# Tensor, vector and scalar engine of a streaming-encoder mixer: from program order to the scheduler's order

## Chip, cores, metric

The kernel runs on one core of a Trainium2 chip. The metric is the device time of one execution in microseconds (us); the time of a kernel is the median of several runs.

## What is computed

The reference is one hybrid encoder block on 1024 frames of width 1024 with 16 learned meta tokens in front, all in float32. A token mixer of eight heads (four mLSTM heads, four retention heads) is followed by a gated MLP with a causal convolution:

```
h = concat(meta, x)
u = rmsnorm(h) ; proj = u @ w_in          # q, k, v, output gate of 4 + 4 heads
q, k: convolution + silu (mLSTM)  or  rotary (retention)
per chunk of a head:  out = (q k^T * decay) v + q C ;  C = decay * C + k^T v
h = h + (gate * head_norm(out)) @ w_out
h = h + (silu(dwconv(rmsnorm(h) @ w_up)) * (rmsnorm(h) @ w_gate)) @ w_down
out = rmsnorm(h)[16:]
```

The state C makes the nine chunks of a head a serial chain; the heads are independent of one another.

## The kernel before, in words

**Stages.** The norm of the input, the projections of head 4's value and query and the sums of activation blocks come first. Then the mixer runs over the heads in the order 4, 0, 1, 2, 3, 5, 6, 7, three pairs after the first head (line 1521, `for p, (a, b) in enumerate(PAIRS)`). The output projection, the gated MLP and the final norm follow.

**The projections.** A projection of a head is a unit of seven block products (a Strassen-like scheme, `wino_fm` at L742 and `v_steps` at L788). Each product is split in chunks; one step is 12 matmuls of a group (L671 high weight times high input, L672, L673) into a PSUM bank of tag `pa` or `pb` (two banks each), and the bank is then copied out or added by `evac` (L734: ACT at L736 and L738, DVE at L740). A unit has 14 such evacuations. A float32 weight is used as a high and a low part: ACT casts the high part (L292), DVE subtracts for the low part (L295), after DVE has made sums of weight quarters (L368, L369, L372, L373).

**The scan.** For each chunk, `scan_a` (L1248) makes the scores on PE (L1255, L1260), then ACT scales the keys (L1271) and DVE the scores (L1274 to L1279). `scan_b` (L1282) makes state update and numerator on PE (L1302, L1304, L1306), then DVE updates the state (L1315), ACT copies the numerator out (L1317) and DVE takes its statistics (L1321). `post_steps` (L1325) normalises with a square root on ACT (L1340, L1342) and L1350, transposes on PE into the one bank `tr` (L1359), multiplies by norm weight and gate on DVE into one of three buffers `mx` (L1367) and stores that to DRAM (L1379, SP). The banks `sA`, `num`, `upd` and `tr` exist once each.

**Emission.** The order in which the program is written down is itself a plan. `slot` (L1417) emits one projection step and then up to two side tasks (scan pieces, convolutions, gates, table work), as long as estimated loads of DVE and ACT are not too far ahead of PE's; `tick` (L257) emits the evacuations of the step before and one piece of each pending weight split; `drain` (L1432) emits what is left of a head before its buffers are used again. `m_unit` (L396) folds two rows of the output weights and adds the result to DRAM (L420 on SP, L422 on POOL); its raw buffer is one of the four into which all later weights are loaded (L222, SP).

**Who orders the engines.** Line 2203 builds the program with `schedule_with_timeline_sim=True`: the framework's scheduler walks the emitted program over a modelled timeline, and an engine whose earliest instruction isn't ready there may take a later one that is. The resulting order is fixed at compile time; on the chip each engine follows it. A hook (L91 to L97) sees every instruction as it is emitted:

```
    def watch(ins):
        nm, kind = ins.engine.name, type(ins).__name__
        if nm not in RATE or not ins.outs or "DMA" in kind or "Tile" in kind:
            return
        if pinned[0] and nm in before:
            tc.add_manual_dep(ins, before[nm], mybir.DependencyInfo(mybir.DependencyClass.NoSync, mybir.DependencyReason.DATA), reason="order")
        before[nm] = ins.name
```

`RATE` names PE, DVE and ACT. While `pinned[0]` is true, each instruction of these engines depends, for its order alone and with no semaphore, on the one emitted before it on its engine: the engine keeps the order of emission. The rest of the hook keeps the load estimates and doesn't look at `pinned`. DMA issues on SP and POOL and the POOL memsets (L801) are never held.

`pinned[0]` is set true at L1520, after the seven products of head 4's output gate with head 4's first side tasks (`go(o_steps(4))`, L1519), and false at L1601, after the last scan of head 7 and the first six of the output projection's steps (`drain("end")`, L1599). All before L1520 and after L1601 goes by the scheduler's order.

Of the kernel before, what the change touches and what calls it, by code (L numbers as in the profile page):

```python
# [65 lines left out]
def body(ctx, tc, h_in, vecs, cst, mask_in, rot, w_v0, w_vp, w_g, w_out, w_up, w_gate, w_down, out):  # L66
# [19 lines left out]
    pinned = [False]  # L86
# [686 lines left out]
    def o_steps(h):  # L773
        return wino_fm("o", h, OC, fm_dst([sigt[:, 0], sigt[:, 1]], KEEP))
# [653 lines left out]
    def go(steps, pe=1):  # L1428
        for m in steps:
            slot(m, pe=pe)  # L1430
# [86 lines left out]
        return [(lambda: tables_load(h), 0, lambda: "gates" in done)]  # L1517
    reset()
    go(o_steps(4))  # L1519
    pinned[0] = True  # L1520
    for p, (a, b) in enumerate(PAIRS):
        side += sig_tasks(prev) if p else sig_tasks(4)
        side += rest[0] + loads_of(a)
# [684 lines left out]
```

## Time and profile before

| | |
|---|---|
| time, median of 3 runs | 1673.84 us (1672.29 to 1673.98) |
| the profiled execution's own time | 1665.56 us |
| its span, first to last instruction | 1663.6 us |
| PE busy | 1520.7 us, 91% |
| DVE busy | 1131.5 us, 68% |
| ACT busy | 761.0 us, 46% |
| mean granted TensorE clock | 0.961 |
| DMA moved | 232.16 MB, mean 140 GB/s |

The profile is of one execution. Busy time of an engine is the time in which it had an instruction; PE's own ends are modelled. The views used below are: busy time of each engine by stretches of the span; the sums of waits, where a row `PE tr L1359 <- DVE mx L1367: 23.7, 11, 6.3` says that PE's instruction of line 1359 writing `tr` stood idle until line 1367 on DVE had ended, 23.7 us in 11 cases, the longest 6.3; and the timeline, which gives start, duration, engine, line, operation, tiles (out<-in) and in square brackets the idle time before an instruction with its releaser. SPq is the queue of DMA issues on SP. The part of the span with held order lies between about 121 us (end of L1519's steps) and about 837 us.

### The profile page before, as it was taken

Reading aid. Unit: us, or ns where it says so; the run is one execution under the profiler, and the core shown is the slowest. Engines: PE = TensorE matmul, PEld = TensorE weight load, DVE = VectorE, ACT = ScalarE, POOL = GpSimd, SP = SyncE. Lnnn points to the kernel's source line nnn. Section 1 sums busy time; section 2 is a strip of 40 time slices with the busy share of each in tenths; the row PEclk is TensorE's granted clock in tenths of the full one; section 3 lists DMA queues with packets and bytes.
Section 4 is the critical chain, followed back from the end, with each engine's and each line's share of the span. In section 5 each row is a group of like instructions: output and inputs, shape, how many; then the busy total and the mean of one; then the engine's idle time right before and its main releaser. Section 6 shows DMA issues by size and latency. Waiting matters only on the chain.

```text
span 1663.6 us, 25278 instructions
## 1 busy us (share of the span) xinstructions
PE 1520.7 (91%) x9799; PEld 1375.4 (83%) x9799; DVE 1131.5 (68%) x2161; ACT 761.0 (46%) x1494; POOL 67.5 (4%) x104
## 2 busy tenths in 40 slices
PE   5988897798987999989779999999999999999998
PEld 4878786697986998888658899899999999888887
DVE  6685666566765776766377777877666666677757
ACT  5344543454563444454324545644444444444444
POOL 0000000000000000000000000022221000000000
PEclk9999998999998999999979999999999999999999
DMA  6013235442453425459644321788776222863312
GB/s 213 26 52 103 64 111 161 109 153 77 106 186 84 162 85 159 129 180 318 231 151 132 120 89 66 233 212 211 205 191 162 82 76 77 294 213 108 99 53 102
DMA packets 107175, 232.16 MB, mean 140 GB/s; under 512 B 10808, under 2 KB 34048, under 8 KB 106880
## 3 DMA queue, kind: packets, MB, share of 16 engines
q1 hardware_dynamic: 96736, 201.12, 36.6%
q0 software_dynamic: 10176, 29.37, 9.2%
q8 instruction: 76, 1.25, 0.3%
q14 instruction: 43, 0.35, 0.1%
q10 hardware_dynamic: 144, 0.07, 0.0%
HBM read 179.10 MB, written 74.49 MB: 152 GB/s over the span
## 4 chain that ended last, share of the span: by engine, by line
PE 69%; DVE 10%; DMA 8%; ACT 7%; issue 5%; SPq 0%; DVEq 0%; POOLq 0%; ACTq 0%
PE pdx L671 2%; PE pdx L672 2%; PE pdx L673 2%; PE pup_x L672 2%; PE pup_x L673 2%; PE pga_x L672 2%; PE pup_x L671 2%; PE pga_x L673 2%; PE pga_x L671 2%; PE pdy L672 2%; PE pdy L671 2%; PE pdy L673 2%; PE pwx L673 2%; PE pwx L671 2%; PE pwx L672 2%
## 5 line engine op out<-in xcount | busy, mean ns | idle before, releaser
L575 ACT CAST hi_up<-raw_up 128x512 fp32r<-128x512 f32 (+1 forms) x52 | 36.4, 719 | 106.0 <-PE pga_z L672 61.2
L671 PE MATMUL pup_x<-uh_g,hi_up 128*128 128x256 f32 (+1 forms) x240 | 67.1, 282 | 1.2 <-ACT uh_g L1612 1.2
L576 DVE TENSOR_TENSOR lo_ga<-fraw_ga,hi_ga 128x512 fp32r<-128x512 f32 (+1 forms) x52 | 41.9, 808 | 37.6 <-ACT hi_ga L575 37.4
L672 PE MATMUL pup_x<-ul_g,hi_up 128*128 128x256 f32 (+1 forms) x240 | 67.1, 281 | 0.1
L1321 DVE BATCH_NORM_STATS2 bn<-n 128x6 f32<-128x256 f32 (+1 forms) x72 | 30.8, 428 | 53.1 <-ACT den L1319 33.6
L673 PE MATMUL pup_x<-uh_g,lo_up 128*128 128x256 f32 (+1 forms) x240 | 66.4, 282 | 0.0
L576 DVE TENSOR_TENSOR lo_up<-raw_up,hi_up 128x512 fp32r<-128x512 f32 (+1 forms) x52 | 41.2, 808 | 35.7 <-ACT hi_up L575 34.9
L576 DVE TENSOR_TENSOR lo_d<-rd,hi_d 128x1024 fp32r<-128x1024 f32 (+1 forms) x34 | 37.7, 1112 | 32.9 <-ACT hi_d L575 32.8
L672 PE MATMUL pdx<-ul_d,hi_d 128*128 128x512 f32 (+1 forms) x156 | 58.1, 375 | 0.0
L673 PE MATMUL pdx<-uh_d,lo_d 128*128 128x512 f32 (+1 forms) x156 | 57.6, 373 | 0.0
L575 ACT CAST hi_ga<-fraw_ga 128x512 fp32r<-128x512 f32 (+1 forms) x52 | 36.4, 719 | 46.3 <-PE pup_z L672 24.0
L575 ACT CAST hi_d<-rd 128x1024 fp32r<-128x1024 f32 (+1 forms) x34 | 32.3, 960 | 49.0 <-PE pdy L672 32.6
L672 PE MATMUL pdy<-ul_d,hi_d 128*128 128x512 f32 x132 | 51.9, 393 | 0.0
L673 PE MATMUL pdy<-uh_d,lo_d 128*128 128x512 f32 x132 | 51.3, 389 | 0.0
L671 PE MATMUL pdx<-uh_d,hi_d 128*128 128x512 f32 (+1 forms) x156 | 48.8, 374 | 0.0
L671 PE MATMUL pdy<-uh_d,hi_d 128*128 128x512 f32 x132 | 48.3, 392 | 0.0
L672 PE MATMUL pga_x<-ul_g,hi_ga 128*128 128x512 f32 x120 | 47.6, 397 | 0.0
L673 PE MATMUL pga_x<-uh_g,lo_ga 128*128 128x512 f32 x120 | 47.3, 394 | 0.0
L671 PEld LDWEIGHTS pup_x<-uh_g,hi_up 128*128 128x128 f32 x240 | 45.3, 189 | 2.3 <-ACT uh_g L1612 1.4
L671 PE MATMUL pga_x<-uh_g,hi_ga 128*128 128x512 f32 x120 | 47.1, 393 | 0.0
L672 PEld LDWEIGHTS pup_x<-ul_g,hi_up 128*128 128x128 f32 x240 | 45.4, 189 | 1.1 <-DVE ul_g L1613 0.3
L673 PEld LDWEIGHTS pup_x<-uh_g,lo_up 128*128 128x128 f32 x240 | 44.6, 188 | 0.8
(1679 smaller groups left out, 5892.5 us busy)
## 6 DMA issues: line engine op xcount, KB each, us to landing
raw_up<-w_up_d SPq DMA_DIRECT2D x22, 512.0 KB, 4.4
fraw_ga<-w_gate_d SPq DMA_DIRECT2D x22, 512.0 KB, 4.2
acts<-cv SPq DMA_DIRECT2D x44, 256.0 KB, 4.1
wsd<-w_down_d POOLq DMA_DIRECT2D x44, 256.0 KB, 6.2
rd<-wsd SPq DMA_DIRECT2D x22, 512.0 KB, 3.6
raw_w<-w_out_d SPq DMA_DIRECT2D x20, 512.0 KB, 4.8
wsw<-raw_w SPq DMA_DIRECT2D x32, 256.0 KB, 3.9
raw_m<-w_out_d SPq DMA_DIRECT2D x14, 512.0 KB, 3.7
```

Source lines behind the costliest of these rows:

```text
L575: AC.copy(hi[:, o:o + n], x)
L576: V.tensor_tensor(lo[:, o:o + n], x, hi[:, o:o + n].bitcast(F32), ALU.subtract)
L671: m.append(PE.matmul(pt, ah, xh_, start=first and k == 0, stop=False, skip_group_check=True))
L672: PE.matmul(pt, ah, xl_, start=False, stop=False, skip_group_check=True)
L673: m.append(PE.matmul(pt, al, xh_, start=False, stop=last and k == n - 1, skip_group_check=True))
L1321: V.bn_stats(sb[:L], pn[:L, :DV])
```

## The change

One word. The order of emission, the load estimates that steer it, all operands, buffers and DMAs stay.

```
     go(o_steps(4))
-    pinned[0] = True
+    pinned[0] = False
     for p, (a, b) in enumerate(PAIRS):
```

With it the three engines get the scheduler's order in the whole program.

## Prediction

> **What bounds the kernel now.** I read the page first, then busy time by stretches, then what PE waited for inside the part whose order is held (121 to 837 us), and last the timeline around single stalls. The page:
>
> ```profile
> span 1663.6 us, 25278 instructions
> ...
> PE 1520.7 (91%) x9799; PEld 1375.4 (83%) x9799; DVE 1131.5 (68%) x2161; ACT 761.0 (46%) x1494; POOL 67.5 (4%) x104
> ```
>
> PE is the bound. Busy time by stretches (us of the stretch, then busy time of PE, weight loads, DVE, ACT, POOL, the granted clock, DMA):
>
> ```profile
> 121.00:837.00 716.00, 621.74 (x4456) 579.99 (x4455) 462.83 (x1030) 335.65 (x726) 11.62 (x20) 0.94 0.47 143
> ...
> 837.00:1663.00 826.00, 808.80 (x4685) 711.01 (x4685) 582.13 (x964) 371.81 (x679) 55.55 (x79) 0.99 0.48 143
> ```
>
> After the mixer PE is idle for 17.2 of 826 us, in the mixer for 716 - 621.74 = 94.3 of 716, or 13.2%, and its clock is 0.94 there against 0.99. Everything that the change can move lies in these 94.3 us and in what new idle time it makes: PE's work stays 621.74 us. What ended PE's waits there, in total, times, longest:
>
> ```profile
> PE tr L1359 <- DVE mx L1367: 23.7, 11, 6.3
> PE s L1255 <- ACT kT L911: 11.3, 4, 4.1
> PE n L1304 <- DVE bn L1321: 9.6, 6, 4.4
> PE pq5x L671 <- ACT hi_o L292: 9.3, 1, 9.3
> PE pq2x L671 <- ACT hi_o L292: 8.3, 1, 8.3
> PE v L842 <- ACT n L1263: 8.1, 1, 8.1
> ...
> PE po6y L671 <- DVE sig L740: 0.2, 1, 0.2
> ```
>
> The reader is to see two things. The waits are few and long, and they come from places where one head ends and the next begins. And the projections hardly wait for their banks to be emptied: po6y's 0.2 us is one of the two such rows, both 0.2. By the code the held part has 18 units with 14 evacuations each, 252 in all, so a handoff of a bank costs PE 0.4 / 252, nothing.
>
> **The change part by part.** It adds and removes no instruction, no DMA and no semaphore by itself; it lets PE, DVE and ACT take a later instruction where the scheduler's timeline finds the earlier one not ready. That has a good side and a bad side, and each is priced from a place of this trace.
>
> *What is given back.* An engine held to order stands still while later work is ready behind the waiting instruction. DVE near 373 us:
>
> ```profile
> 372.58 0.62 DVE L1367 SCALAR_TENSOR_TENSOR mx<-tr,vec,sig 128x384 f32<-128x384 f32 x1 [1.12 <-PE tr L1359]
> 378.90 0.62 DVE L1367 SCALAR_TENSOR_TENSOR mx<-tr,vec,sig 128x384 f32<-128x384 f32 x1 [5.70 <-DMA mxd<-mx]
> 379.43 1.22 DVE L368 TENSOR_TENSOR raw_vp<-raw_vp,raw_vp 128x1024 f32<-128x1024 f32 x1
> ```
>
> For 5.70 us DVE waits until a store has freed one of the three mx buffers, and only then makes the weight sum of L368 that stood behind. Set free, it would make the sum first, and PE would run projection steps while a transpose waits for the bank tr. I count the row tr <- mx, 23.7 us, as what can be filled, because projection matmuls with weights already split follow those transposes, and take three quarters of it: -18 us. The waits for kT, bn and n (11.3 + 9.6 + 8.1 us) are links of a serial chain with casts of the same moment behind them; pq5x and pq2x (9.3 + 8.3 us) wait for a weight that is still being loaded into a buffer which the accumulation into DRAM has to leave first:
>
> ```profile
> SPq L222 <- DMA accd<-raw_m: 106.6, 12, 23.0
> ```
>
> That is a matter of SP's and POOL's queues. Their order isn't held before either, but it comes from the same modelled timeline, so it moves with the engines: an accumulation that is ready earlier there goes out earlier, or a load is queued behind a store that is late. I bound this by these two waits on the one side (-17.6) and by one more wait as long as the longest of the row on the other (+23.0), and take 0, since both signs have the same ground. If all six rows quoted above went, it would be 70.3 us; with PE at the clock of the later stage the mixer would save another 621.74 x 0.05 = 31 us. That is the far end of the good side, -101; its near end is 0.
>
> *What it costs.* The trace holds a place where the same kind of work already runs in the scheduler's order: head 4's output gate, 75 to 121 us, with side tasks between its steps. PE's waits there:
>
> ```profile
> PE po4x L671 <- ACT sig L736: 3.7, 1, 3.7
> PE po4x L671 <- DVE sig L740: 3.1, 2, 2.2
> PE po4x L672 <- DVE uS2l L1494: 1.4, 1, 1.4
> ```
>
> The first two rows are the handoff of a bank, 6.8 us for the unit's 14 evacuations, 0.49 us each, against nothing in the held part. Why, is seen in the order. PE takes one matmul of the third product (uS2h) ahead of the second and the first product's other chunk:
>
> ```profile
> 88.73 0.28 PE L671 MATMUL po4x<-uS2h,hi_o 128*128 128x258 f32 x1
> 88.86 0.28 PE L671 MATMUL po4y<-u12h,hi_o 128*128 128x256 f32 x1
> ...
> 90.39 0.36 PE L671 MATMUL po4x<-u11h,hi_o 128*128 128x256 f32 x1
> ```
>
> and ACT fills its time with casts, one of them for the next head (raw_q0a), in front of the copy that empties PE's bank:
>
> ```profile
> 92.22 1.28 ACT L954 ACT_TABLE_LOAD   x1
> 93.52 0.36 ACT L954 ACTIVATE gates<-pg,gsm 36x128 f32<-36x128 f32 x1
> 93.78 0.60 ACT L292 CAST hi_o<-raw_o4a 128x512 fp32r<-128x512 f32 x1
> 94.29 0.62 ACT L292 CAST hi_o<-raw_q0a 128x512 fp32r<-128x512 f32 x1
> 94.81 0.61 ACT L292 CAST hi_o<-raw_o4a 128x512 fp32r<-128x512 f32 x1
> 95.33 0.36 ACT L736 COPY sig<-po4x 128x256 f32<-128x256 f32 x1
> ```
>
> ```profile
> 91.74 0.28 PE L673 MATMUL po4x<-u11h,lo_o 128*128 128x256 f32 x1
> 95.74 0.38 PE L671 MATMUL po4x<-uS2h,hi_o 128*128 128x256 f32 x1 [3.72 <-ACT sig L736]
> ```
>
> The bank was full at 92.0 and emptied at 95.7. Where the modelled timeline has the end of a matmul group later than the chip, or a cast earlier, an evacuation is put behind long foreign pieces (0.6 us a cast, 1.28 a table load), and in the fixed order it stays there. DVE was busy for 41.76 of the 46 us between 75 and 121, and that is what makes such a place dear: nine of the 48 stretches of 15 us between 120 and 840 have DVE busy 12 us or more; the first and the last of them:
>
> ```profile
> 210.00:225.00 15.00, 15.00 (x120) 14.68 (x119) 12.47 (x26) 6.89 (x17) 0.00 (x0) 1.00 0.12 36
> ...
> 750.00:765.00 15.00, 14.08 (x115) 13.66 (x115) 14.08 (x25) 5.49 (x12) 0.00 (x0) 1.00 0.75 268
> ```
>
> In them I price an evacuation as in the freed place: 252 x 9 / 48 = 47 of them by 0.49 us, +23 us. The other 205 lie between 0 (the held rows) and 0.49 us (the freed ones); I take a fifth, 0.1 us, nearer to the held rows, since DVE and ACT have spare time there: +20 us. Ends of the bad side: 0 and 252 x 0.49 = +123. The handoffs of the scan (two for each of 72 chunks) get no price of their own: their waits in the held part are in the rows above, and late copies of the numerator are the same mechanism.
>
> *Sum.* -18 + 0 + 23 + 20 = +25 us on the profiled execution's 1665.56 us, that is 1690.6. That execution lies 8.3 us under the median of the runs, 1673.84; the forecast is of a median, so **1673.8 + 25 = 1699 us**.
>
> [...]
>
> **The rivals.**
>
> *Faster: standing time is given back and little is lost.* For it speaks that every long wait above has ready work behind it, and that the stage after the mixer runs in the scheduler's order with PE idle for 2% only. Against it speak the rows of head 4's output gate, and that the later stage has no serial scan. It decides once less than 18 us are lost to late evacuations. With the first three rows and v given back by half (52.7 / 2 = 26), and nothing lost: 1673.8 - 26 = **1648 us**; with all six rows and the clock it could reach 1573, which I don't believe because of the serial chains.
>
> *No change: the order hardly differs.* If on the modelled timeline the held instructions are seldom late, the free choice picks the same ones. For it: the emission is already spaced by estimated loads. Against it: the order at 88.73 shows that the choice is used. **1674 us**.
>
> *Much slower: functions of ACT are mixed.* The square roots of the statistics come in 24 pieces (8 heads, 3 each) and now cost 11 loads:
>
> ```profile
> L1340 ACT ACT_TABLE_LOAD x6 | 7.7, 1283 | 0.1
> ...
> L1342 ACT ACT_TABLE_LOAD x5 | 6.4, 1283 | 0.1
> ```
>
> If free choice sets each between exponentials and silus, it takes a load for it and one back: 48 x 1.283 = 62 us on ACT, 48 more than now with 7 of the other loads counted in. ACT is busy 335.65 of 716 us, so half of it may be hidden: +24 beside the +25, and with evacuations at 0.2 us instead of 0.1 another +20: 1673.8 + 69 = **1743 us**. For it: ACT's order at 92.22, a load in front of the evacuation. Against it: the pieces of one function are emitted in one go.
>
> **How the numbers follow.** Forecast 0.52, much slower 0.20, faster 0.20, no change 0.08. The forecast's own spread is 1678 (5 us net) to 1730 (a third of the 123 more). The lower end of the range is 1652, which leaves out about half of the faster case, 0.11; the upper end 1765, half way between much slower and the +123 with the queues' +23 and half of the 62, leaves out about 0.08. A change of 0.2% (3.3 us) is about what a measurement of this kernel can tell from none. Faster by more than that 0.20, within it 0.08, slower 0.72.
>
> **What would show it.** Right: in the stretch of the mixer PE's idle time rises from 94 to about 119 us; the waits of PE for sig, raw, v (L736, L738, L740) rise from 0.4 to some 40 us; the row tr <- mx falls to about 6; table loads in the mixer stay near those now. Wrong: PE's waits for evacuations stay under 10 us (then the bad side was mis-sized), tr <- mx doesn't fall (then nothing was in hand behind it), or the idle time goes to weights that SP's queue brings late, which would make the queues' 0 the failed term. If the order on the engines turns out nearly that of before, the premise fails.

## The result

The changed kernel takes **1600.7 us** (median of 4 runs, 1598.8 to 1605.5) against 1673.1 us before: a ratio of 0.957, 95% interval 0.955 to 0.960. The forecast was 1699 us, slower, with a range of 1652 to 1765. The sign was wrong and the time lies outside the range.

### The profile after

The page of the changed kernel, the lines that answer to those shown of before:

```profile
span 1603.7 us, 25323 instructions
...
PE 1511.2 (94%) x9799; PEld 1368.9 (85%) x9799; DVE 1112.6 (69%) x2161; ACT 778.6 (49%) x1506; POOL 67.5 (4%) x104
```

The matmuls are the same 9799. ACT has 12 instructions more, all of them table loads. Busy time by stretches (stretch, PE, weight loads, DVE, ACT, POOL, granted clock, DMA):

```profile
121.00:777.00 656.00, 610.80 (x4461) 570.72 (x4460) 443.40 (x1030) 353.85 (x742) 11.53 (x20) 0.97 0.49 151
777.00:1603.00 826.00, 808.93 (x4706) 712.26 (x4704) 585.06 (x968) 372.60 (x679) 55.64 (x79) 0.99 0.49 144
```

The stage behind the mixer is as long as before, 826 us with 808.9 busy. The mixer took 716 us and takes 656: the whole difference of the two spans, 59.9 us, is there (777 us is set so that the rest is as long as before). PE's idle time in it fell from 94.3 to 45.2 us (49 us), and its busy time from 621.7 to 610.8 us (11 us) with the clock up from 0.94 to 0.97. (The medians are 72 us apart; the profiled execution of before lies 8 us under its median and that of after 5 us above.) What PE waits for now, us in total, times, longest:

```profile
PE n L1304 <- DVE bn L1321: 7.6, 5, 3.2
PE u L1302 <- DVE C L1315: 7.2, 2, 4.2
PE pwy L672 <- DVE rr L1030: 6.7, 1, 6.7
PE n L1304 <- DVE z L1336: 6.3, 3, 3.9
PE pq2x L671 <- ACT hi_o L292: 3.5, 1, 3.5
PE pq0x L671 <- ACT rawq L736: 3.5, 1, 3.5
...
PE pq5x L671 <- ACT hi_o L292: 0.8, 1, 0.8
...
PE tr L1359 <- DVE mx L1367: 0.5, 1, 0.5
```

The row that led before, tr <- mx with 23.7 us, is 0.5 us. The two waits for the weights of heads 5 and 2, 9.3 and 8.3 us, are 0.8 and 3.5. New is a row such as pq0x <- rawq, 3.5 us: a bank not yet emptied. All waits of PE from 121 us to the first MLP matmul (980 us before, 921 after), sorted by what PE was about to do (matmuls of a projection that waited for a weight part, or for a bank; transposes into tr; scan pieces; the output projection):

| PE waits, us | before | after |
|---|---|---|
| weights of the projections | 23.6 | 4.3 |
| banks of the projections | 0.4 | 9.5 |
| bank tr | 28.4 | 5.6 |
| scan pieces | 35.4 | 23.6 |
| output projection | 9.5 | 10.0 |
| other | 3.9 | 0 |
| sum | 101.2 | 52.9 |

How a weight came late is seen on ACT around head 2's first weight. Before, ACT's timeline:

```profile
322.40 0.37 ACT L736 COPY sig<-po1x 128x256 f32<-128x256 f32 x1 [1.08 <-PE po1x L673]
333.05 0.62 ACT L292 CAST hi_o<-raw_q2a 128x512 fp32r<-128x512 f32 x1 [10.27 <-DMA raw_q2a<-w_g_d]
```

For 10.27 us ACT stood at this cast; the scan's copies behind it stood too (the next numerator was complete at 323.7 us and was copied out at 334.09). After:

```profile
302.47 1.28 ACT L778 ACT_TABLE_LOAD   x1
303.77 1.06 ACT L778 ACTIVATE sig<-sig 128x1026 f32<-128x1026 f32 x1
304.73 0.35 ACT L736 COPY sig<-po1x 128x256 f32<-128x256 f32 x1
305.12 1.06 ACT L778 ACTIVATE sig<-sig 128x1026 f32<-128x1026 f32 x1
306.08 0.36 ACT L1317 COPY v<-n 128x256 f32<-128x256 f32 x1
...
310.44 0.20 ACT L1340 ACTIVATE z<-z 128x4 f32<-128x4 f32 x1
313.99 0.62 ACT L292 CAST hi_o<-raw_q2a 128x512 fp32r<-128x512 f32 x1 [3.34 <-DMA raw_q2a<-w_g_d]
```

ACT fills the time with two sigmoid passes, scan copies and a square root, and the cast comes when the weight is there. The load itself is issued 19.9 us sooner by the clock; SP's queue before, then after:

```profile
328.37 0.33 SPq L222 DMA_DIRECT2D raw_q2a<-w_g_d  x1
```

```profile
308.46 0.33 SPq L222 DMA_DIRECT2D raw_q2a<-w_g_d  x1
```

Seen from PE this weight comes no earlier, though: PE ends the unit before it, po1, 21.2 us sooner too (303.9 against 325.1), and starts pq2 10.8 us after that end, 8.6 before. PE's wait is shorter, 3.5 us against 8.3, because PE has scan matmuls in the first 7 us of the gap, while ACT copies the scan's numerators out. For head 5 the weight does come earlier: pq5 starts 2.2 us after po3's end, 10.6 before.

What the load waits for is the accumulation of the folded output weights into DRAM, whose buffer it takes (SP's queue stood for it 21.9 us before and 5.2 us after). The accumulation is issued on POOL, before and then after:

```profile
322.84 1.95 POOL L422 DMA_DIRECT2D accd<-raw_m  x2 [37.46 <-DVE raw_m L416]
```

```profile
303.19 0.87 POOL L422 DMA_DIRECT2D accd<-raw_m  x1 [0.85 <-DVE pt L1274]
```

The load follows it by 5.5 and 5.3 us, so the queues add the same in both kernels. Before, POOL stood until DVE's part of the fold (L416) was done.

### The profile page after: what moved, and what is told of

The parts are those of the page before. It is cut to its first block, busy times and chain, and to the rows that moved or that the text cites. A ratio compares the mean times of both kernels' runs of the same rounds, so it can differ in the third digit from the quotient of the medians.

```text
span 1603.7 us, 25323 instructions
## 1 busy us (share of the span) xinstructions
PE 1511.2 (94%) x9799; PEld 1368.9 (85%) x9799; DVE 1112.6 (69%) x2161; ACT 778.6 (49%) x1506; POOL 67.5 (4%) x104
## 4 chain that ended last, share of the span: by engine, by line
PE 71%; DMA 12%; DVE 9%; issue 4%; ACT 4%; SPq 0%; POOL 0%; DVEq 0%; POOLq 0%; ACTq 0%
DMA accd<-raw_m 3%; PE pdx L671 3%; PE pdx L672 3%; PE pdx L673 3%; PE pup_x L672 2%; PE pup_x L673 2%; PE pga_x L672 2%; PE pup_x L671 2%; PE pga_x L673 2%; PE pga_x L671 2%; PE pdy L672 2%; PE pdy L671 2%; PE pdy L673 2%; PE pwx L672 2%; PE pwx L671 2%
## 5 line engine op out<-in xcount | busy, mean ns | idle before, releaser
L575 ACT CAST hi_d<-rd 128x1024 fp32r<-128x1024 f32 (+1 forms) x34 | 32.3, 960 | 48.9 <-PE pdy L672 32.6
```

Of the source, the lines that this page charges most:

```text
L575: AC.copy(hi[:, o:o + n], x)
```

## The experiments

All ratios are to runs of the kernel before on the same chip; the medians come from several chips, so the ratios are what is compared. Theory A: the standing time sat on ACT and DVE. Theory B: PE's own freedom makes the gain. Theory C: all share it.

### One engine held, two free

The hook holds only the engines named:

```
-        if pinned[0] and nm in before:
+        if pinned[0] and nm in before and nm in ('PE',):
```

**PE held.** 

> PE alone is held to the order of emission in the mixer; DVE and ACT are free. Theory A (the standing time sits on ACT and DVE, whose waiting instruction keeps ready casts, sums and copies behind it; PE only suffers): most of the 72 us gain stays, 1610 to 1625 us. Theory B (PE's own freedom to run projection steps while a transpose or a scan piece is late makes the gain): most is lost, 1650 to 1670 us. Theory C (the engines share it, the gains do not add up): 1630 to 1645 us.

**DVE held.** 

> DVE alone is held. Theory A: DVE's waits for ACT and for the store buffers hold weight sums again, 1635 to 1660 us. Theory B: nearly as fast as with all free, 1600 to 1612 us. Theory C: 1625 to 1645 us.

**ACT held.** 

> ACT alone is held. Theory A: casts that wait for a load keep copies and evacuations behind them again, 1635 to 1660 us. Theory B: nearly as fast as with all free, 1600 to 1612 us. Theory C: 1625 to 1645 us.

### One engine free, two held

**PE free.** 

> PE alone is free in the mixer, DVE and ACT are held. Theory D (a weight goes from its load through ACT's cast and DVE's sums and back to the queue of loads, so ACT and DVE only help when both are free; PE alone can't shorten that chain): 1668 to 1685 us. Theory E (what a free PE takes early is evacuated late by engines that keep to the order of emission): slower than with one more engine free, 1690 to 1710 us. Theory B (PE's own freedom counts): 1640 to 1655 us.

**DVE free.** 

> DVE alone is free, PE and ACT are held. Theory D: little, 1665 to 1680 us. Theory E: the same, since PE keeps the order for which the other engines are placed. If each engine gave its own share (the 72 us in three parts): 1645 to 1655 us.

**ACT free.** 

> ACT alone is free, PE and DVE are held. Theory D: little, 1665 to 1680 us. Theory E: the same. If each engine gave its own share: 1645 to 1655 us.

Measured, all eight cases:

| free | median us | ratio, 95% interval |
|---|---|---|
| none (before) | 1673 | 1 |
| PE | 1714.4 | 1.025 (1.022 to 1.029) |
| DVE | 1681.2 | 1.006 (1.004 to 1.008) |
| ACT | 1662.1 | 0.994 (0.990 to 0.998) |
| PE, DVE | 1692.4 | 1.010 (1.007 to 1.013) |
| PE, ACT | 1689.4 | 1.007 (1.005 to 1.009) |
| DVE, ACT | 1640.1 | 0.978 (0.975 to 0.982) |
| all (after) | 1600.7 | 0.957 (0.955 to 0.960) |

No theory had this table. One free engine alone is worth little (ACT, 0.6%) or less than nothing. By the ratios ACT and DVE together bring 2.2%, and PE, which alone costs 2.5% and beside ACT 1.3%, brings another 2.1% once both are free. Theories A and B fall as written; C named the size with PE held (1630 to 1645) but not that holding DVE or ACT alone would end above the kernel before. D and E expected the same for DVE and ACT, little, and both times lie just outside their 1665 to 1680 us, so these two runs do not tell them apart. For PE, E's direction came out (its 1690 to 1710 was 4 us low), and its reason was tested next. With ACT held, PE's waits:

```profile
PE pwx L671 <- ACT hi_w L575: 12.7, 2, 12.3
PE pq5x L671 <- ACT hi_o L292: 10.1, 1, 10.1
PE pq2x L671 <- ACT hi_o L292: 10.0, 1, 10.0
```

The two waits for weights that fell to 0.8 and 3.5 us with all free are back at 10; with DVE held they are 10.8 and 7.3. A weight's path is load, cast on ACT, sums and low part on DVE, and the buffer is free for the next load only then.

### Why PE alone loses

With PE alone free, its waits for banks, sorted as in the table further up, are 36.1 us (0.4 before) and for weights 36.9 us (23.6 before). First the banks:

```
+    def evac(n, d, q):
+        loose[0] = True
...
+        loose[0] = False
```

where an instruction emitted while `loose[0]` is true is not held and holds nothing.

> As with PE alone free (1714 us), but ACT's and DVE's 252 evacuations of projection banks are let out of the held order too. Theory E (PE takes projection steps early, and the held engines empty the banks only in the order of emission; 36 us of PE's waits there): the waits for evacuations fall under 10 us and the time to 1675 to 1695 us. If the weight splits, still held, cost as much whatever happens to the banks: 1700 to 1715 us.

Measured: 1710.5 us, 1.023 (1.020 to 1.027). PE's waits for banks fell to 5.8 us, as asked for, and the time did not: the waits for weights rose to 48.9 us. Theory E falls as the cause; late evacuation alone does not make the loss. The trace of PE alone free says who stands where. ACT's waits there, then before:

```profile
ACT kw L1271 <- PE s L1260: 46.8, 27, 4.1
ACT v L1317 <- PE n L1306: 42.7, 29, 3.9
```

```profile
ACT v L1317 <- PE n L1306: 28.9, 26, 2.6
ACT kw L1271 <- PE s L1260: 24.9, 16, 5.3
```

and DVE's wait for the transposes, in the same order:

```profile
DVE mx L1367 <- PE tr L1359: 55.2, 23, 5.4
```

```profile
DVE mx L1367 <- PE tr L1359: 19.2, 17, 2.0
```

A free PE puts projection matmuls ahead of the scan's matmuls and transposes; ACT and DVE, held, stand at the scan's next piece 72 us longer in these three rows, with casts and evacuations behind it (all rows up to the first matmul of the output projection). So the scan's pieces on ACT and DVE were let out (`@loosely` sets `loose[0]` around scan_a, scan_b, stats and half), casts, sums and evacuations staying held:

> As with PE alone free (1714 us), but the scan's pieces on ACT and DVE (scan_a, scan_b, statistics, gating) are let out of the held order; casts, sums, evacuations and the rest stay held. Theory G (a free PE puts projection matmuls ahead of scan pieces, the held ACT and DVE stand at the scan's next piece, 73 us more than before, and casts and evacuations wait behind it): PE's waits for weights and banks, 37 and 36 us, fall by half or more and the time to 1635 to 1670 us. If it isn't the scan behind which they stand: 1695 to 1715 us.

Measured: **1619.5 us**, 0.968 (0.966 to 0.971), below even what theory G expected: 95 us under PE alone free. PE's waits for weights are 12.8 us and for banks 17.3 us. Theory G's forecast came out: with the scan out of the held order the loss is gone, and more (42 us were lost, 95 come back). Its reason is shown for DVE, whose row falls from 55.2 to 14.1 us. ACT's two rows stay at 39.1 and 35.9 us, but ACT is no longer held to them. The edit also lets scan pieces go ahead of casts and sums; no run lets the scan out with PE held, so how much of the 95 us is which stays open.

### The weights alone

> As before, all three engines held, but the preparation of weights (ACT's casts, DVE's sums and low parts, the folding of the output weights in m_unit) is let out of the order. Theory F (weights come late because their pieces stand behind waiting scan pieces on ACT and DVE): PE's waits for weights fall from 33 to under 15 us and the time to 1640 to 1656 us. If the gain needs PE's freedom as well: 1662 to 1685 us.

Measured: 1653.1 us, 0.989 (0.985 to 0.993). PE no longer waits for a weight of a projection at all; what leads is what led before:

```profile
PE tr L1371 <- DVE mx L1379: 24.1, 12, 5.0
PE s L1267 <- ACT kT L923: 12.9, 4, 3.6
```

(12 lines of code more, so L1379 is L1367 of before.) Theory F is right, and the term is sized for an order otherwise held: 16 us. The accumulation for head 2 is issued at 306.15 us there and the load again 5.5 us behind it.

### The fold of the output weights

```
-                    while busy():
-                        yield
```

(both places in m_unit, all engines held)

> All engines held as before; in m_unit the two waits for a lull of DVE and ACT are taken out, so that the folding of the output weights is emitted without gaps. If the late second half of a fold (13 us after the first near 306 us) makes the two waits of 8.3 and 9.3 us for the weights of heads 2 and 5: both waits fall under 3 us and the time to 1655 to 1662 us. If the load waits for something else that comes as late: 1670 to 1678 us.

Measured: 1671.2 us, 0.9995 (0.997 to 1.002). The time is that of the second case, but not for its reason: both waits for weights are gone, and nothing was gained. PE's waits:

```profile
PE po1y L667 <- ACT sig L734: 13.9, 1, 13.9
PE po3y L667 <- ACT sig L734: 13.3, 1, 13.3
```

ACT's timeline there:

```profile
307.78 0.37 ACT L734 ACTIVATE sig<-po1x 128x256 f32<-128x256 f32 x1
322.79 0.62 ACT L292 CAST hi_o<-raw_q2a 128x512 fp32r<-128x512 f32 x1 [14.64 <-DMA raw_q2a<-w_g_d]
323.31 0.65 ACT L734 ACTIVATE sig<-po1y 128x256 f32<-128x256 f32 x2
```

The load did come sooner (issued at 318.7 us instead of 328.4), but the cast that waits for it now stands in front of the evacuations of po1y. In this held order the earlier fold turned a wait for a weight into a longer one for a bank.

### The place from which the price was taken

```
     reset()
+    pinned[0] = True
     go(o_steps(4))
     pinned[0] = False
```

> The other way round: all three engines are held through head 4's output gate (the place from which the prediction priced late evacuations) and free in the mixer. If the scheduler's order costs 6.8 us of late evacuations there, as the prediction read it: 1592 to 1596 us, with PE's waits for sig in that stage gone. If those waits come from DVE being nearly full there, whatever the order: 1599 to 1608 us, and the same stage is no shorter.

Measured: 1618.3 us, 0.965 (0.961 to 0.968), neither of the two: 10 to 18 us slower than with that place free, by ratios and by medians. PE's waits in it, held:

```profile
PE pe L981 <- DVE gates L974: 13.1, 1, 13.1
PE po4y L671 <- DVE sig L740: 9.6, 1, 9.6
```

Held, PE stands at the gates' products with projection steps behind them. The last matmul of head 4's output gate ends at 149 us instead of 121, and the waits for its banks come to 13.7 us, where the changed kernel has 5.3 and the kernel before, free there too, 6.8.

### Versions of the changed kernel

**More side tasks a step** (`lim=6.0, most=4`). 

> The changed kernel, with the emission's own spacing loosened: up to four side tasks a step instead of two, until DVE and ACT are 6 us ahead instead of 2.5. If the free order does the spacing by itself: 1590 to 1605 us. If side tasks emitted earlier take precedence over projection steps and DVE becomes the bound in places: 1610 to 1640 us.

Measured: 1603.3 us, 0.959 (0.955 to 0.962): no change. This much of the emission's spacing makes no difference once the order is free.

**Earlier folds.** 

> The changed kernel without the two waits for a lull in m_unit. If the weights of heads 2 and 5 (3.5 and 0.8 us of PE's waits left) are late for want of an earlier fold: 1595 to 1599 us. If not: 1599 to 1604 us.

Measured: 1596.9 us, 0.955 (0.952 to 0.959). Once more, beside the changed kernel:

> The changed kernel without the two waits for a lull in m_unit, once more, beside the changed kernel on the same chip: 3 to 5 us under it if the first look (1596.9 us) holds, within 2 us if it was chance.

> The same, and without the two waits for a lull in w_unit as well (the block sums of the output weights). If these waits only serve a held order: 1590 to 1598 us. If DVE gets too much at once: 1600 to 1610 us.

> The changed kernel itself, as the measure for the two beside it: 1598 to 1604 us.

Measured on one chip: 1595.0 us without m_unit's waits (0.955, 0.952 to 0.958), 1596.6 us without w_unit's too (0.956, 0.953 to 0.958), 1603.6 us the changed kernel (0.959, 0.957 to 0.961). Both comparisons put the first of them ahead of the changed kernel, by 4 and 9 us; the intervals still overlap, so it is likely, not certain, that it is faster. The edit that gave nothing in the held order seems to give a little in the free one.

## Why the prediction was wrong

**The bound and its place: right, but for the clock.** What changed lies in the mixer, 49 us of it in its 94.3 us of idle time. The clause that PE's work stays 621.74 us failed: it was 610.80, and the clock had been counted only in the far end of the good side.

**What is given back, the bank tr: right.** -18 us forecast, -22.8 measured. With PE alone held the row tr <- mx is still 18.7 us, so PE's own freedom has a part in it, as the step said.

**The queues, taken as 0: wrong.** The step said that the waits for pq5x and pq2x are a matter of SP's and POOL's queues, with the same ground for both signs. The path it named, a load behind an accumulation, is right, but what it waited for was ACT and DVE: before, POOL's 37.46 us of idle time ended with the fold on DVE, and the load came 5.3 to 5.6 us after the accumulation in four traces (before, after, weights let out, earlier folds in the held order). Part of the fold's lateness was its place in the emission (with earlier folds the load goes out at 318.7 us instead of 328.4), part its standing behind other pieces (311.6 with the weights' preparation let out). That preparation alone, every queue unheld as before, removed all waits for weights. In the changed kernel the two waits fell by 13.3 us, one of them because PE had other work in the gap, and all waits for weights by 19.3; the term lies near its bound of -17.6, not at 0.

**The serial links, taken as 0: wrong in part.** The scan's waits fell by 11.8 us, the others by 3.9. Before, foreign work stood in the chain, as the cast of 333.05 us in front of the numerator's copy; no run sizes this by itself.

**What it costs, +43: wrong, and it decided the sign.** The mechanism exists: banks are emptied later, 9.5 us of waits against 0.4. The size was off by more than four times, because the price came from one place (0.49 us an evacuation in head 4's output gate), and the step read its waits as the cost of free order. Held, the same place ends 27 us later than in the changed kernel and its waits for banks are 13.7 us against 5.3. So the order was not what they cost; that a full DVE (41.76 of 46 us) makes them is likely, but was not tried by itself. The nearest row was near in kind of work but not a comparison; there was no row of the same place held. With 9.1 in place of 43 the sum would have been some 9 us faster, not 25 slower. Waits for evacuations under 10 us were one of the prediction's own signs of being wrong; they are 9.5.

**The rivals.** "Faster" had the right mechanism and 0.20; its 1648 us stopped at half of 52.7 us, without weights and clock. The argument against it, that the later stage has no serial scan, was sound: PE stays idle for 6.9% of the mixer against 2% there, and the scan's waits are the largest class left, 23.6 us. "Much slower" by table loads: the loads did grow, 34 to 46 in the whole program. In the changed mixer the square roots' rows are

```profile
L1340 ACT ACT_TABLE_LOAD x10 | 12.8, 1283 | 0.2
...
L1342 ACT ACT_TABLE_LOAD x6 | 7.7, 1283 | 0.1
```

16 loads against 11. Twelve more loads are 15.4 us on an engine busy for 353.85 of 656 us, and the time fell all the same. Around the load at 302.47 us the copy ahead ends at 302.45 and the sigmoid behind it starts 1.30 us after the load began: there the load took ACT its own 1.28 us and 0.02 us on either side.

Two sums of the working do not come out of their own terms: the upper end by the terms named would be 1797, not 1765, and a third of the 123 above the forecast is 1740, not 1730. The time lies under the range, so neither decided anything.

**The sum as it came out**, in waits of PE: tr -22.8, weights -19.3, scan -11.8, other -3.9, output projection +0.5, banks +9.1, together -48.2 us; with 11 us less of PE's busy time, which goes with the clock's 0.94 to 0.97, it is 59 of the 59.9 us of the spans. Why the clock rose was not shown: the runs have only the mean clock of a stretch, 0.94 with PE idle for 13.2% of the mixer before and 0.97 with 6.9% after.

## What to carry to other kernels

Price an order by what stands behind each waiting instruction, on the helper engines first: the waits of PE that were followed to their source here (head 2's weight, 8.3 us, and po1y in the run with earlier folds, 13.9 us) were an ACT queue whose head waited for a load while scan copies and evacuations stood behind it. Free an engine together with those that serve it: here PE free alone (1.025), with DVE (1.010) or with ACT (1.007) was slower than none free, and gained only with both (0.957, against 0.978 without PE). When a shorter wait is found, look whether its cause came earlier or whether the engine had other work in the gap. And take a price from a place only when the same place is known both ways; head 4's output gate showed waits for its banks in either order, 13.7 us held and 5.3 to 6.8 us free.

## What was not expected of the hardware

Nothing in the durations: a cast of 128x512 took 0.60 to 0.62 us and a table load 1.28 us in the rows shown of both kernels. The engines' strictness was: on ACT, a ready copy of the scan stood some 10 us behind a cast whose load was late (ACT idle for 10.27 us), and ACT stood 14.64 us in the run with earlier folds; in both places ACT ran its queue from the head alone, so that in the second one late load reached PE as a wait for an unrelated bank of 13.9 us.
